# SBUF offsets of the matmul operands in a two-layer trunk: all tiles at one offset modulo 512 bytes

## The chip, the cores and the metric

The kernel runs on one core of a Trainium2 chip. The metric is the device time of one execution in microseconds (us), the median of several runs. Lower is better. A profile is one execution recorded by the hardware profiler; its span runs from the first to the last instruction of the program.

## The reference

A sequence of 512 tokens, 1024 wide, goes through two layers. Each sub-layer's output is added to `alpha * h` and normalised. Layer 0 mixes tokens with a Mamba-2 scan (SSD), layer 1 with stick-breaking attention; each is followed by an MLP with a squared ReLU and 4096 hidden units.

```
for layer in range(DEPTH):                 # DEPTH = 2
    if layer < N_A_LAYERS:                 # layer 0
        mix = mamba2_mixer(h, w_in, conv_w, ..., w_out)
    else:                                  # layer 1
        k, v = shared_kv(h, sb_w_k, sb_w_v)
        mix = stick_breaking_attention(h, sb_w_q, k, v, sb_w_o)
    h = layer_norm(DEEPNORM_ALPHA * h + mix, ...)
    h = layer_norm(DEEPNORM_ALPHA * h + square(relu(h @ w1)) @ w2, ...)
```

All values are float32.

## The kernel before

**Precision.** Every float32 matrix is split into a high part (float32r) and a low part, and every product is three matmuls: high by high, high by low, low by high. This is `mm3`, lines 207 to 209. Nearly every line of TensorE in the profile is one of these three. Each matmul has a stationary operand of 128 x 128 and a moving operand of up to 512 columns, both read from SBUF. The stationary one is brought in by an instruction of its own, the weight load (PEld in the profile).

**Weights.** `stream` lists 272 weight pieces of 128 x 1024 float32 in the order of use. `emit_w` (lines 150 to 194) fetches piece number i into a raw tile (`wr`), ScalarE copies it to the high part `wh` (L190), VectorE or GpSimd subtracts to get the low part `wl` (L192). In the MLPs a second pool lends buffers: with `e = 2` extra ones, four pieces in a row go to the pool `wp`, the next two to the pool of the MLP, and so on (`use = ... i % (4 + e) >= 4`).

**Stages and their span in the trace.** SSD 0 to 471 us, MLP of layer 0 to 806, attention to 1100 (with the first part of the next MLP's work woven in), MLP of layer 1 to the end. Each MLP goes through the hidden units in four quarters q. First eight pieces of W1 give `f` (stationary `wh`/`wl`, moving the normalised activations `ln_hh`/`ln_hl`): 192 matmuls of 512 columns (in quarter 0 four pieces are done in halves of 256 columns). Then seven block products `P1` to `P7` with W2 (stationary the hidden activations `hP`/`lP`/`l`, moving `wh`/`wl`) are summed in the banks `X`, `Y`, `Z`, `V`: 168 matmuls of 512 columns. A scheduler sets the order of the instructions of each engine and the semaphores.

**Places in SBUF.** Each partition is filled from byte 16512 on, pool by pool, every tile rounded up to 32 bytes. In the kernel before this gives (last column: start modulo 512; every slice that a matmul reads starts a whole multiple of 512 bytes after its tile's start):

| pool | tiles | first byte | modulo 512 |
|---|---|---|---|
| `cp` | `ones_r`, `ident`, `tri_le`, `tri_gt`, `none_r`, `ntri_ge` | 16512 | 128 |
| `cp` | `mhalf` (4 bytes), `cw`, `cbias`, `hv`, `nw` | 19584 | 128 and others |
| `ap` | activations: `x_h`, `ln_hh`, `ln_hl`, `yT`, `R`, `L` (the `l` of the products), `v`, `o_h` | 20704 | 224 |
| `wp` | raw tiles, `wh`, `wl` (four buffers each) | 102624 | 224 |
| `lp` | `st`, `mv`, `rs`, `sm`, `nm`, `sq` of the norms: 608 bytes in all | 143584 | 224 and others |
| `sp`, `mlp0`, `att`, `mlp1`, one after the other | SSD: conv, `W`, `xd`, `bt`, `xe`, `yg`; MLP: `hP`, `lP`, lent `wh`/`wl`; attention: `q`, `k`, `sp`, `w`, `vp` | 144192 | 320 |

In the last SSD projection (`so`), two weight pieces lie in the free SSD buffers `xd`, `dx` and `yg` and are called `wx`, `wdx` and `wyg` in the profile; they are at 320, the pieces called `wh` and `wl` beside them at 224.

So each of the 7414 matmuls has a pair of offsets, moving and stationary. Of the 4566 matmuls of 512 columns 2672 have 224 and 224, 416 have 320 and 320, 14 have 128 and 128, and 1464 have two different ones (1216 moving 224 with stationary 320, 152 the other way round, 96 moving 320 with stationary 128). Of these 1464, 480 are `f` of the MLPs (twenty lent pieces of 24 matmuls, ten in each MLP), 816 are products of the MLPs, and 168 lie outside: 48 in `so`, 24 in the output projection of attention, 96 single ones between others. The 2848 shorter matmuls have equal offsets in 2272 cases and different ones in 576.

Of the kernel before, what the change touches and what calls it, by code (L numbers as in the profile page):

```python
# [11 lines left out]
F32 = mybir.dt.float32  # L12
# [5 lines left out]
P = 128  # L18
# [3 lines left out]
NT = T // P  # L22
DI = 2048
G = 8
H = 32
# [10 lines left out]
def trunk(ctx: ExitStack, tc: tile.TileContext, io):  # L36
    nc = tc.nc

    cp = ctx.enter_context(tc.tile_pool(name="cp", bufs=1))
    ap = ctx.enter_context(tc.tile_pool(name="ap", bufs=5))  # L40
    wp = ctx.enter_context(tc.tile_pool(name="wp", bufs=4))
    lp = ctx.enter_context(tc.tile_pool(name="lp", bufs=2))
# [11 lines left out]
    def f(x):  # L54
        return x.bitcast(F32)

    nc.scalar.preload_act_table_set("natural_log_exp_and_others")
    ones_r = cp.tile([P, P], F32R, name="ones_r")
    one = f(ones_r)
    nc.vector.memset(one, 1.0)  # L60
    warm = psum("bg", [P, 4, P], "warm")
    for _ in range(14):
# [11 lines left out]
    ntri_ge = cp.tile([P, P], F32R, name="ntri_ge")  # L74
    nc.gpsimd.affine_select(ntri_ge, f(none_r), pattern=[[-1, P]], compare_op=ALU.is_ge, fill=0.0,
                            base=0, channel_multiplier=1)
    mhalf = cp.tile([P, 1], F32, name="mhalf")
    nc.gpsimd.memset(mhalf, -0.5)
    cw = cp.tile([P, 32, 4], F32, name="cw")
    cb_ = cp.tile([P, 32], F32, name="cbias")  # L80
    hv = cp.tile([P, 3, H], F32, name="hv")
    nw = cp.tile([P, 16], F32, name="nw")

    stream = []
    marks = []
# [60 lines left out]
    sums = {}  # L146
# [75 lines left out]
    class Filler:  # L222
        def __init__(self):
            self.queue = []
            self.left = 0.0
# [85 lines left out]
    class Norm:  # L311
        def __init__(self, v, idx, name, final=False):
            self.v, self.idx, self.name, self.final = v, idx, name, final
            self.sums = idx % 2 == 1
            self.st = lp.tile([P, NT, 2, 6], F32, tag="st", name=f"{name}_st", bufs=2)
            self.mv = lp.tile([P, NT, 2], F32, tag="mv", name=f"{name}_mv", bufs=2)
            self.rs = lp.tile([P, NT], F32, tag="rs", name=f"{name}_rs", bufs=2)
            if self.sums:
                self.sm, self.nm, self.sq = (lp.tile([P, NT, w], F32, tag=f"s{w}{n}", name=f"{name}_{n}", bufs=1)
                                             for n, w in (("sm", 2), ("nm", 1), ("sq", 2)))  # L320
                self.junk = None
            self.hl = None
            self.rows = None

# [954 lines left out]
```

## Time and profile before

| | us |
|---|---|
| median of 3 runs (1435.85 to 1437.47) | 1436.23 |
| the profiled execution's time | 1436.23 |
| its span, first to last instruction | 1434.2 |
| TensorE busy (matmuls) | 1406.7 (98%) |
| VectorE busy | 1078.6 (75%) |
| ScalarE busy | 783.8 (55%) |
| GpSimd busy | 221.5 (15%) |

[...] What sets TensorE's pace is the distance from one start to the next, which is read from the timeline: the starts of the first matmul of a stretch and of the first one behind it, and how many lie between. Starts are printed to 0.01 us.

### The profile page before, as it was taken

How to read it: one execution, taken by the hardware profiler on the slowest of the kernel's cores; microseconds unless marked ns; L12 is line 12 of the kernel's file. 1: busy time of each engine (PE TensorE's matmuls, PEld its weight loads, DVE VectorE, ACT ScalarE, POOL GpSimd, SP SyncE). 2: the span in 40 equal slices, each digit the busy share in tenths (PEclk: the TensorE clock that was granted, in tenths of full speed). 3: DMA queues.
4: the chain of work that ended last, by engine and by line, in shares of the span. 5: the costliest groups of instructions: out<-in, count | busy, mean ns of one | idle time of the engine just before them, and what ended most of it. 6: DMA issues, size and time to landing. Idle time of an engine off the chain costs nothing. (4 is left out here: it accounts for less than half of the span.)

```text
span 1434.2 us, 19323 instructions
## 1 busy us (share of the span) xinstructions
PE 1406.7 (98%) x7414; PEld 1200.9 (84%) x7414; DVE 1078.6 (75%) x1530; ACT 783.8 (55%) x1264; POOL 221.5 (15%) x249
## 2 busy tenths in 40 slices
PE   9999999999999999999999999999999999999997
PEld 6898897889997988888888789899879888888885
DVE  5798898368877696866759768787867966758587
ACT  5556574246652453636345468898833635354453
POOL 2344554135453100000000200000000000000001
PEclk9999999999999999999999999999999999999998
DMA  5223222221223455455453421121223454454533
GB/s 184 74 77 130 74 60 73 88 89 60 74 75 102 133 161 177 127 181 154 141 161 105 145 89 45 48 71 51 82 74 118 132 186 151 147 165 140 166 111 122
DMA packets 46699, 162.99 MB, mean 114 GB/s; under 512 B 5520, under 2 KB 5776, under 8 KB 46608
## 3 DMA queue, kind: packets, MB, share of 16 engines
q1 hardware_dynamic: 44016, 157.44, 35.1%
q10 hardware_dynamic: 2592, 4.33, 0.9%
q8 instruction: 58, 0.95, 0.3%
q14 instruction: 33, 0.27, 0.1%
HBM read 159.65 MB, written 2.10 MB: 113 GB/s over the span
## 5 line engine op out<-in xcount | busy, mean ns | idle before, releaser
L190 ACT CAST wh<-wr 128x1024 fp32r<-128x1024 f32 x235 | 246.6, 1050 | 336.1 <-DMA wr<-w 162.7
L192 DVE TENSOR_TENSOR wl<-wr,wh 128x1024 fp32r<-128x1024 f32 x218 | 268.3, 1232 | 181.7 <-ACT wh L190 180.7
L208 PE MATMUL f<-ln_hl,wh 128*128 128x512 f32 (+1 forms) x544 | 202.4, 373 | 0.0
L209 PE MATMUL f<-ln_hh,wl 128*128 128x512 f32 (+1 forms) x544 | 202.4, 373 | 0.0
L207 PE MATMUL f<-ln_hh,wh 128*128 128x512 f32 (+1 forms) x544 | 201.6, 373 | 0.0
L208 PEld LDWEIGHTS f<-ln_hl,wh 128*128 128x128 f32 x544 | 102.5, 189 | 18.7
L209 PEld LDWEIGHTS f<-ln_hh,wl 128*128 128x128 f32 x544 | 102.5, 189 | 18.6
L207 PEld LDWEIGHTS f<-ln_hh,wh 128*128 128x128 f32 x544 | 102.1, 189 | 18.7
L346 POOL TENSOR_TENSOR ln_rs<-ln_sq 128x1 f32<-128x1 f32 (+1 forms) x6 | 3.1, 510 | 643.5 <-ACT lnr L344 643.5
L207 PE MATMUL X<-wh,hP 128*128 128x512 f32 x192 | 75.6, 394 | 0.0
L208 PE MATMUL X<-wl,hP 128*128 128x512 f32 x192 | 75.5, 393 | 0.0
L209 PE MATMUL X<-wh,l 128*128 128x512 f32 x192 | 74.9, 393 | 0.0
L209 PE MATMUL pz<-wh,x_l 128*128 128x256 f32 x256 | 72.7, 284 | 0.0
L208 PE MATMUL pz<-wl,x_h 128*128 128x256 f32 x256 | 72.5, 283 | 0.0
L207 PE MATMUL pz<-wh,x_h 128*128 128x256 f32 x256 | 72.4, 283 | 0.0
L458 ACT CAST hP<-r 128x512 fp32r<-128x512 f32 x80 | 48.0, 619 | 31.2 <-DVE r L470 30.3
L192 POOL TENSOR_TENSOR wl<-wr,wh 128x1024 fp32r<-128x1024 f32 x17 | 42.5, 2502 | 93.8 <-ACT wh L190 93.4
L207 PE MATMUL px<-x_h,wh 128*128 128x512 f32 x128 | 50.7, 396 | 0.0
L208 PE MATMUL Y<-wl,hP 128*128 128x512 f32 x128 | 50.4, 394 | 0.0
L209 PE MATMUL px<-x_h,wl 128*128 128x512 f32 x128 | 50.2, 393 | 0.0
L208 PE MATMUL px<-x_l,wh 128*128 128x512 f32 x128 | 50.2, 392 | 0.0
L207 PE MATMUL Y<-wh,hP 128*128 128x512 f32 x128 | 49.8, 394 | 0.0
(1365 smaller groups left out, 3936.5 us busy)
## 6 DMA issues: line engine op xcount, KB each, us to landing
wr<-w SPq DMA_DIRECT2D x160, 512.0 KB, 3.6
wr<-w_bc SPq DMA_DIRECT2D x16, 512.0 KB, 3.5
wr<-w_x SPq DMA_DIRECT2D x16, 512.0 KB, 3.5
wr<-w_z SPq DMA_DIRECT2D x16, 512.0 KB, 3.6
wr<-w_so SPq DMA_DIRECT2D x16, 512.0 KB, 3.6
rawa<-w SPq DMA_DIRECT2D x16, 512.0 KB, 3.6
rawc<-w SPq DMA_DIRECT2D x16, 512.0 KB, 4.6
wr<-w_qk SPq DMA_DIRECT2D x16, 512.0 KB, 3.6
```

The lines of the kernel that those rows point to most:

```text
L190: nc.scalar.copy(hi, raw)
L192: eng.tensor_sub(lo, raw, f(hi))
L207: nc.tensor.matmul(out, a[0], b[0], start=start, stop=False, skip_group_check=skip)
L208: nc.tensor.matmul(out, a[0], b[1], start=False, stop=False, skip_group_check=skip)
L209: return nc.tensor.matmul(out, a[1], b[0], start=False, stop=stop, skip_group_check=skip)
L346: nc.gpsimd.tensor_add(rs, self.sq[:, t0:t1, 0], self.sq[:, t0:t1, 1])
L458: nc.scalar.copy(h, src)
```

## The change

Nothing is computed in another way. The small constants move ahead of the constant matrices, and the tiles of the norms take another shape and number, so that their sizes add up differently:

```
     nc.scalar.preload_act_table_set("natural_log_exp_and_others")
+    mhalf = cp.tile([P, 1], F32, name="mhalf")
+    cw = cp.tile([P, 32, 4], F32, name="cw")
+    cb_ = cp.tile([P, 32], F32, name="cbias")
+    hv = cp.tile([P, 3, H], F32, name="hv")
+    nw = cp.tile([P, 16], F32, name="nw")
     ones_r = cp.tile([P, P], F32R, name="ones_r")
...
-    mhalf = cp.tile([P, 1], F32, name="mhalf")
     nc.gpsimd.memset(mhalf, -0.5)
-    cw = cp.tile([P, 32, 4], F32, name="cw")
-    cb_ = cp.tile([P, 32], F32, name="cbias")
-    hv = cp.tile([P, 3, H], F32, name="hv")
-    nw = cp.tile([P, 16], F32, name="nw")
...
             self.sums = idx % 2 == 1
-            self.st = lp.tile([P, NT, 2, 6], F32, tag="st", name=f"{name}_st", bufs=2)
-            self.mv = lp.tile([P, NT, 2], F32, tag="mv", name=f"{name}_mv", bufs=2)
             self.rs = lp.tile([P, NT], F32, tag="rs", name=f"{name}_rs", bufs=2)
             if self.sums:
-                self.sm, self.nm, self.sq = (lp.tile([P, NT, w], F32, tag=f"s{w}{n}", name=f"{name}_{n}", bufs=1)
-                                             for n, w in (("sm", 2), ("nm", 1), ("sq", 2)))
+                x = lp.tile([P, NT, 14], F32, tag="sums", name=f"{name}_sums", bufs=1)
+                self.sm, self.nm, self.sq = x[:, :, 0:2], x[:, :, 2:3], x[:, :, 4:6]
                 self.junk = None
+            else:
+                self.st = lp.tile([P, NT, 2, 6], F32, tag="st", name=f"{name}_st", bufs=1)
+                self.mv = lp.tile([P, NT, 2], F32, tag="mv", name=f"{name}_mv", bufs=1)
```

What it does to the places: the six constant matrices start at 17632 (224 modulo 512) instead of 16512 (128). `ap` and `wp` stay where they were. `lp` holds 512 bytes instead of 608, so that the pools of the stages start at 144096 (224) instead of 144192 (320). In the changed program all 7414 matmuls have a moving and a stationary operand at 224. A few tiles that no matmul reads have other offsets before and after: `yl` and `sz` of the SSD, the sums of the norms.

What it does to the program: nothing else. On each of the five engines the built programs have the same instructions in the same order with the same waits and the same semaphore updates; only addresses differ, and `sm`, `nm` and `sq` are called `sums` with a step of 56 bytes from token tile to token tile.

## Rows read from the trace of the kernel before

**Rows 1.** The page, part 1: span, and busy time of each engine.

```profile
span 1434.2 us, 19323 instructions
PE 1406.7 (98%) x7414; PEld 1200.9 (84%) x7414; DVE 1078.6 (75%) x1530; ACT 783.8 (55%) x1264; POOL 221.5 (15%) x249
```

**Rows 2.** Table by stretch: us, busy time (count) by engine, granted clock, DMA share, GB/s.

```profile
600.00:700.00 100.00, 100.00 (x436) 81.65 (x435) 74.37 (x90) 48.18 (x64) 0.00 (x0) 1.00 0.47 146
```

**Rows 3.** Waits of PE over the span: us, times, longest; the first row.

```profile
PE ln_b L394 <- DVE v L430: 2.5, 1, 2.5
```

**Rows 4.** Timeline, last SSD projection, weights in two pools: start, duration, line, tiles.

```profile
453.06 0.39 PE L207 MATMUL so<-wh,yT4h 128*128 128x512 f32 x1
...
457.82 0.40 PE L207 MATMUL so<-wx,yT4h 128*128 128x512 f32 x1
...
460.64 0.39 PE L207 MATMUL so<-wdx,yT4h 128*128 128x512 f32 x1
```

**Rows 5.** Timeline, W1 of quarter 1, MLP of layer 0: two lent pieces, then four others.

```profile
567.66 0.39 PE L207 MATMUL f<-ln_hh,wh 128*128 128x512 f32 x1
...
578.91 0.39 PE L207 MATMUL f<-ln_hh,wh 128*128 128x512 f32 x1
...
600.67 0.40 PE L207 MATMUL X<-wh,hP 128*128 128x512 f32 x1
```

**Rows 6.** Timeline of the weight loads at the start of the four pieces.

```profile
578.91 0.19 PEld L208 LDWEIGHTS f<-ln_hl,wh 128*128 128x128 f32 x1
```

**Rows 7.** Timeline, the products `V` (P2) and `Y` (P3) of quarter 1.

```profile
629.78 0.40 PE L207 MATMUL V<-wh,hP 128*128 128x512 f32 x1
...
634.00 0.39 PE L207 MATMUL Y<-wh,hP 128*128 128x512 f32 x1
...
639.46 0.39 PE L207 MATMUL f<-ln_hh,wh 128*128 128x512 f32 x1
```

**Rows 8.** Timeline, starts of the products of quarters 0, 2, 3 and the row behind.

```profile
517.83 0.40 PE L207 MATMUL X<-wh,hP 128*128 128x512 f32 x1
...
556.76 0.40 PE L207 MATMUL f<-ln_hh,wh 128*128 128x512 f32 x1
...
683.38 0.39 PE L207 MATMUL X<-wh,hP 128*128 128x512 f32 x1
...
722.48 0.39 PE L207 MATMUL f<-ln_hh,wh 128*128 128x512 f32 x1
...
766.75 0.40 PE L207 MATMUL X<-wh,hP 128*128 128x512 f32 x1
...
805.68 0.38 PE L394 MATMUL ln_b<-ident,v 128*128 128x128 f32 x2
```

**Rows 9.** Timeline, products of quarter 0 in the MLP of layer 1.

```profile
1135.47 0.40 PE L207 MATMUL X<-wh,hP 128*128 128x512 f32 x1
...
1174.39 0.40 PE L207 MATMUL f<-ln_hh,wh 128*128 128x512 f32 x1
```

**Rows 10.** Timeline, matmuls of 256 columns: the gate projection of the SSD.

```profile
100.06 0.28 PE L209 MATMUL pz<-wh,x_l 128*128 128x256 f32 x1
...
101.48 0.28 PE L209 MATMUL pz<-wh,x_l 128*128 128x256 f32 x1
```

**Rows 11.** Timeline, matmuls of attention with a constant matrix as the stationary operand.

```profile
903.19 0.28 PE L1120 MATMUL z<-sp200l,ntri_ge 128*128 128x256 f32 x1
903.31 0.22 PE L1120 MATMUL z<-sp200h,ntri_ge 128*128 128x128 f32 x1
```

**Rows 12.** Groups of VectorE, 495 to 805 us: count, busy us, mean ns, idle before.

```profile
L459 DVE TENSOR_TENSOR lP<-r,hP 128x512 fp32r<-128x512 f32 x24 | 16.0, 683 | 0.0
L459 DVE TENSOR_TENSOR l<-r,hP 128x512 fp32r<-128x512 f32 x16 | 10.9, 682 | 1.2 <-ACT hP L458 1.2
```

**Rows 13.** Table by stretch, PE alone: the granted clock behind an idle TensorE.

```profile
241.80:245.20 3.40, 3.40 (x9) 0.50 0.51 154
```

## The prediction

> **What bounds the kernel now.** First the busy times: TensorE has matmuls in flight in 98% of the span, the next engine, VectorE, is at 75% [rows 1]. Then the table by stretch: in the MLP from 600 to 700 us TensorE is busy in all 100 us, at the full granted clock (1.00), with 436 matmuls, and VectorE has a quarter of its time left [rows 2]. Then the waits: the longest that TensorE has in the whole span is 2.5 us, for the rows of a norm, outside the MLPs' flow [rows 3]. So in the MLPs the time is the number of matmuls by the distance from one start to the next. A change of that distance goes into the end one for one; a change on any other engine does not.
>
> The program is the same before and after, instruction by instruction and wait by wait. The one question is whether a matmul's pace hangs on where its operands lie. The timeline answers it, since the kernel before mixes places within a stage. In the last SSD projection, 21 matmuls with `wh`/`wl` (moving at 224, stationary at 224) go from 453.06 to 457.82 us: 4.76 / 21 = 226.7 ns. The 12 behind them take `wx` (moving at 320, same stationary tiles) from 457.82 to 460.64: 235.0 ns [rows 4]. In the MLP, the moving operand stays and the stationary one changes place: 48 matmuls with two lent pieces (320 against 224) take 567.66 to 578.91, 11.25 / 48 = 234.4 ns; the 96 behind them (224 and 224) take 578.91 to 600.67, 21.76 / 96 = 226.7 ns [rows 5].
>
> That alone could mean that 320 is a bad place. The products say no. The 18 matmuls of `V` from 629.78 to 634.00 have moving 224 and stationary 320: 234.4 ns. The 24 of `Y` behind them have **both at 320**: 634.00 to 639.46, 227.5 ns [rows 7]. So it is the relation that counts: equal offsets are fast, different ones slow, by 7 to 8 ns in 227 (3%). A way in which it can come about is in sight: the weight load of the next matmul starts in the same hundredth of a microsecond as the matmul that runs (578.91 in both) and lasts 0.19 us [rows 5, 6], so the two operands are read side by side for most of a matmul. What collides there the trace does not show.
>
> [...]
>
> **The change part by part.** *W1 with lent pieces.* 480 matmuls `f` have different offsets and get equal ones: 480 x (234.4 - 226.7) = 3.7 us [rows 5].
>
> *Products.* A product's stationary operands are partly at 320 (`hP`, `lP`), partly at 224 (`l`), its moving ones at 224 or 320, so stretches of a few matmuls alternate and I cost a whole quarter: 168 matmuls. In the MLP of layer 0 the four quarters take 38.93 us (517.83 to 556.76), 38.79 (600.67 to 639.46), 39.10 (683.38 to 722.48) and 38.93 (766.75 to 805.68), together 155.75 [rows 5, 7, 8]. At 226.7 ns they would take 4 x 168 x 0.2267 = 152.3, at the 227.5 of the equal stretch in [rows 7] 152.9. The saving is 2.9 to 3.4 us. The other MLP repeats it: its first quarter takes 38.92 (1135.47 to 1174.39) [rows 9]. Twice: 5.7 to 6.8; I take 6.3, the middle.
>
> *Outside the MLPs.* 72 long matmuls in runs (`so`, output projection) by 235.0 - 226.7 give 0.6 us [rows 4]; 96 single ones could give 0.8 more. The 576 short ones with different offsets are in doubt: one with scores at 320 and a constant matrix at 128 has 0.12 us to the next start [rows 11], and the gate projection with both at 224 has 12 in 1.42 us, 118 ns [rows 10]. That is no difference within the print; taken at 3 ns either way it is -1.7 to +1.7 us. Outside together: -1.1 to +3.1. Long matmuls among short ones start anew each time, so I take little: 0.5.
>
> *Other engines.* Tiles of ScalarE, VectorE, GpSimd and the DMA queues move from 320 to 224 too. VectorE's `lP` (written at 320) takes 683 ns, its `l` (written at 224) 682 [rows 12]: nothing. The shared tile of sums has the same waits as the three tiles before, and the chain behind the last matmul has the same instructions: nothing.
>
> *Cover.* TensorE that runs 2.5% faster in the MLPs asks for weights 2.5% sooner. VectorE's 74% would be 76% [rows 2], so this costs nothing as long as the weights keep their lead; if not, see the second rival.
>
> Sum: 3.7 + 6.3 + 0.5 = **10.5 us**. The profiled execution took 1436.23 us, 2.0 more than its span, and is the median run; 1436.2 - 10.5 = 1425.7.
>
> **The rivals.** *It is the pool, not the offset.* Tiles at 224 are those of the pools that live for the whole program, tiles at 320 those of the stages' pools, so each fast stretch also has both operands in the same kind of pool. Were it a matter of regions, nothing would change: 1436.2. Against it: in the built program the fast pairs of [rows 5] lie up to some 70,000 bytes apart (`ln_hl` from byte 69856 on, `wl` at 139488), farther than the slow pairs of `V` in [rows 7], some 40,000 (`wh` at 123104, `hP` at 162624), and nothing marks a border at 144192 but the pools' own. [...]
>
> *The supply of weights takes back half.* If TensorE drains the weights faster than the chain of transfer, ScalarE and VectorE refills them, waits come up in the products. TensorE then runs at the pace of the supply, which is no slower than today's: half of the MLPs' gain would remain, about 1431. For it: VectorE at 74%. Against it: a TensorE busy for all of 100 us without a stall [rows 2].
>
> *Equal offsets collide with the other engines (slower).* With everything at 224, TensorE's reads could meet the reads and writes of VectorE and ScalarE, which today work half of the time at another offset. The price if it struck: the 2672 long pairs that are fast now would go from 226.7 to 234.4, 2672 x 7.7 ns = 20.6 us, and the slow ones would gain nothing: 1456.8. The whole is slower by more than 0.2% from the point on where it strikes a seventh of them (2.9 / 20.6). Against it: the 96 fast matmuls of [rows 5] run while both engines write pieces at 224 and at 320 in turn, with no change of pace.
>
> **How the numbers follow.** A measurement here tells 0.2% (2.9 us) from no change. Chances: the forecast 0.84, half taken back 0.06, the pool 0.06, the collision 0.04. The forecast's own range: products and outside at their ends give 3.7 + 5.7 - 1.1 = 8.3 to 3.7 + 6.8 + 3.1 = 13.6. A further doubt is the clock: behind an idle TensorE the granted clock was 0.50 for 3.4 us, which costs 1.7 us of progress [rows 13]; a stretch more or less of these shifts the end by as much. That makes 1422 to 1430, and since half taken back ends just above it and the other two are 0.10 together, this is the range. Faster: 0.84 + 0.06 = 0.90; within 0.2%: 0.06; slower: 0.04.
>
> **What would show it.** In the profile after: the `f` of lent pieces, and `V` of quarter 1, at about 227 ns from start to start, not 234; the products of a quarter in 38.1 to 38.3 us; `so` with `wx` at the pace of `wh`; TensorE still without waits in the MLPs, and durations of VectorE and ScalarE unchanged. The prediction is wrong if `V` stays at 234 with both operands at 224 (then the offset is not the cause), if the fast stretches of today slow down, or if waits for `wh` and `wl` appear in the products.

## The result, and the profile after

| | before | after |
|---|---|---|
| median of four runs each, same chip (us) | 1436.04 (1435.36 to 1437.47) | 1427.18 (1426.70 to 1427.62) |
| ratio after / before | | 0.9937, 95% interval 0.9920 to 0.9954 |
| profiled execution: time, span (us) | 1436.23, 1434.2 | 1426.79, 1424.7 |

The change makes the kernel 8.9 us faster, where 10.5 were forecast; 1427.18 lies inside the range. The page, part 1, of the kernel after stands against [rows 1], and one row of its table by stretch (us, busy time and count by engine, granted clock, DMA share, GB/s) against [rows 2]:

```profile
span 1424.7 us, 19323 instructions
PE 1394.1 (98%) x7414; PEld 1199.9 (84%) x7414; DVE 1078.2 (76%) x1530; ACT 783.9 (55%) x1264; POOL 221.4 (16%) x249
```

```profile
600.00:700.00 100.00, 100.00 (x443) 82.81 (x442) 75.19 (x91) 47.35 (x64) 0.00 (x0) 1.00 0.49 151
```

The busy shares say next to nothing: TensorE is at 98% in both. The count says it: 443 matmuls in the same 100 us instead of 436, at the same clock of 1.00. VectorE, ScalarE and GpSimd work for as long as before, within 0.4 us of some 1078, 784 and 221. So the matmuls of that stretch follow each other more closely on average, while the other engines do the same work.

The timeline of the kernel after (start, duration, engine, line, tiles; lines are one higher than before from the class of the norms on, while `mm3` keeps 207 to 209) shows where. First the last SSD projection, against [rows 4]: 21 matmuls with `wh`/`wl`, then 12 with `wx`, up to the first one with `wdx`.

```profile
452.17 0.39 PE L207 MATMUL so<-wh,yT4h 128*128 128x512 f32 x1
...
456.93 0.39 PE L207 MATMUL so<-wx,yT4h 128*128 128x512 f32 x1
...
459.65 0.39 PE L207 MATMUL so<-wdx,yT4h 128*128 128x512 f32 x1
```

The 21 take 4.76 us as before, 226.7 ns each; the 12 take 2.72, now 226.7 as well, where they took 235.0.

Then W1 of quarter 1 in the MLP of layer 0 (48 matmuls with lent pieces, 96 others), against [rows 5], and in the second piece the products `V` (18) and `Y` (24), against [rows 7].

```profile
565.32 0.39 PE L207 MATMUL f<-ln_hh,wh 128*128 128x512 f32 x1
...
576.20 0.39 PE L207 MATMUL f<-ln_hh,wh 128*128 128x512 f32 x1
...
597.96 0.39 PE L207 MATMUL X<-wh,hP 128*128 128x512 f32 x1
...
626.51 0.39 PE L207 MATMUL V<-wh,hP 128*128 128x512 f32 x1
...
630.59 0.39 PE L207 MATMUL Y<-wh,hP 128*128 128x512 f32 x1
...
636.03 0.39 PE L207 MATMUL f<-ln_hh,wh 128*128 128x512 f32 x1
```

Lent: 10.88 / 48 = 226.7 ns (before 234.4). Others: 21.76 / 96 = 226.7, unchanged. `V`: 4.08 / 18 = 226.7 (234.4). `Y`: 5.44 / 24 = 226.7 (227.5). There is one pace now.

The products of a quarter, against [rows 8]: quarters 0 and 2 from the first row to the second and from the third to the fourth.

```profile
516.36 0.39 PE L207 MATMUL X<-wh,hP 128*128 128x512 f32 x1
...
554.43 0.39 PE L207 MATMUL f<-ln_hh,wh 128*128 128x512 f32 x1
...
679.55 0.39 PE L207 MATMUL X<-wh,hP 128*128 128x512 f32 x1
...
717.63 0.39 PE L207 MATMUL f<-ln_hh,wh 128*128 128x512 f32 x1
```

They take 38.07 and 38.08 us, which is 168 x 0.2267. The table puts the whole span together, from the starts of the matmuls at the borders of the stages (after minus before, us; "again" is a second profile of the same changed kernel, taken later):

| part | after | again |
|---|---|---|
| SSD, up to 471 | -1.12 | -1.63 |
| MLP layer 0: W1, four quarters | -1.89 | -1.89 |
| MLP layer 0: products, quarters 0, 1, 2 | -0.86, -0.71, -1.02 | -0.86, -0.70, -1.02 |
| MLP layer 0: products, quarter 3 | 0.00 | -0.85 |
| attention, to the other MLP | +0.95 | +1.75 |
| MLP layer 1: W1 | -1.77 | -1.78 |
| MLP layer 1: products, quarters 0 to 3 | -0.84, -0.70, -1.02, -0.81 | -0.84, -0.70, -1.02, -0.81 |
| behind the last matmul | +0.35 | +0.33 |

The parts of each column add up to the difference of the unrounded spans, 9.4 and 10.0 us, a little more than lies between the medians. Two lines want an explanation: quarter 3, which gained nothing in one profile and all in the other, and attention, which loses in both.

**Quarter 3.** The products of quarter 3 begin at 761.15. The timeline there shows one wait of TensorE (in brackets: idle before, and who ended it), and VectorE's rows beside it show why.

```profile
764.10 0.39 PE L208 MATMUL X<-wl,hP 128*128 128x512 f32 x1
764.72 0.50 PE L209 MATMUL X<-wh,l 128*128 128x512 f32 x1 [0.23 <-DVE l L460]
```

```profile
762.84 1.22 DVE L192 TENSOR_TENSOR wl<-rawc,wh 128x1024 fp32r<-128x1024 f32 x1
763.98 0.68 DVE L460 TENSOR_TENSOR l<-r,hP 128x512 fp32r<-128x512 f32 x1
```

The low part `l` stood behind a weight piece (`wl`) on VectorE and ended at 764.66. The matmul that needs it started 0.62 us behind its forerunner instead of 0.23, and the next one 0.33 behind it: 0.50 us lost in two distances. In the profile "again" VectorE had it done by 761.84, two us before its matmul came at 763.8, and nothing waits:

```profile
761.16 0.68 DVE L460 TENSOR_TENSOR l<-r,hP 128x512 fp32r<-128x512 f32 x1
```

The rest of the missing 0.85 is at the other end: the last matmul of the quarter starts at 799.53 and the first of the norm behind it at 800.08, 0.32 later than a matmul's distance, since `ln_b` waits for `v` of VectorE. In "again" it follows at a matmul's distance (798.51 to 798.74), and the wait for `v` comes two transposes later, outside the quarter.

**Attention.** All of the loss of the profile after, 0.89 us, is there by 823 us, in the first hundred matmuls behind the MLP. The table by stretch for TensorE alone shows the clock (us, busy time and count, granted clock, DMA share, GB/s), first of the kernel after, then of the kernel before:

```profile
803.40:810.20 6.80, 4.74 (x22) 0.50 0.53 157
```

```profile
811.80:815.20 3.40, 3.40 (x17) 0.50 0.34 117
```

Both kernels let TensorE idle there for the norm. The longest wait is the same one, as [rows 3]:

```profile
PE ln_b L395 <- DVE v L431: 2.5, 1, 2.5
```

Before, 3.40 us of work ran at 0.50, after, 4.74 us. In the timeline of the kernel after, matmuls of 256 columns start 214 ns apart in that stretch (807.44 to 809.79, 11 distances) and 120 ns apart at 1.00 behind it (810.35 to 815.99, 47). Half of the difference, 0.67 us, is taken as lost progress, most of the 0.89: an estimate from the granted 0.50, a little above the 44% that these distances give.

### The profile page after: what moved, and what is told of

The parts are those of the page before. It is cut to its first block, busy times and chain, and to the rows that moved or that the text cites. A ratio compares the mean times of both kernels' runs of the same rounds, so it can differ in the third digit from the quotient of the medians.

```text
span 1424.7 us, 19323 instructions
## 1 busy us (share of the span) xinstructions
PE 1394.1 (98%) x7414; PEld 1199.9 (84%) x7414; DVE 1078.2 (76%) x1530; ACT 783.9 (55%) x1264; POOL 221.4 (16%) x249
## 5 line engine op out<-in xcount | busy, mean ns | idle before, releaser
L347 POOL TENSOR_TENSOR ln_rs<-ln_sums 128x1 f32<-128x1 f32 (+1 forms) x6 | 3.1, 523 | 635.3 <-ACT lnr L345 635.3
L208 PEld LDWEIGHTS pz<-wl,x_h 128*128 128x128 f32 x256 | 48.7, 190 | 0.9
```

Source lines behind the costliest of these rows:

```text
L208: nc.tensor.matmul(out, a[0], b[1], start=False, stop=False, skip_group_check=skip)
L347: nc.gpsimd.tensor_add(rs, self.sq[:, t0:t1, 0], self.sq[:, t0:t1, 1])
```

## The experiments

All are versions of the changed kernel and compute the whole reference. "At X" is the start of an operand modulo 512.

### How far apart, and modulo what

The tile of sums ends the pool `lp`, so its length sets where the pools of the stages start, while `ap` and `wp` stay at 224. Four lengths put `hP`, `lP`, the lent pieces and the rest of the stages' pools at a distance of 32, 64, 128 and 256 bytes from 224. With 16 in place of 14 (d32) they start at 256; with 18 (d64) at 288, with 22 (d128) at 352, with 30 (d256) at 480:

```
-                x = lp.tile([P, NT, 14], F32, tag="sums", name=f"{name}_sums", bufs=1)
+                x = lp.tile([P, NT, 16], F32, tag="sums", name=f"{name}_sums", bufs=1)
```

d32:

> The changed kernel with the tile of sums 32 bytes longer: stage pools at 256 modulo 512, the rest at 224; same instructions and waits. Theory A (operands must agree modulo 512): the lent f pieces of quarter 1 go back from 227 to about 234 ns from start to start, V of quarter 1 too, Y (both at 256) stays at 227; time about 1436. Theory B (the cost grows with the distance of the offsets): about 229 to 230 ns, time about 1430. Theory C (the pool, not the offset): nothing, as in the changed kernel, 1427.

d64:

> Sums 64 bytes longer: stage pools at 288, the rest at 224. Theory A (modulo 512): f lent and V at 234 ns, time about 1436. Theory A64 (agreement modulo 64 is enough): 227 ns everywhere, 1427. Theory B (grows with distance): between d32 and the kernel before, about 232 ns, 1433.

d128:

> Sums 128 bytes longer: stage pools at 352, the rest at 224. Theory A (modulo 512): f lent and V at 234 ns, time about 1436. Agreement modulo 128 is enough: 227 ns, 1427. Theory B: 234 ns or more, 1437.

d256:

> Sums 256 bytes longer: stage pools at 480, the rest at 224, as far apart as 512 allows. Theory A (modulo 512): f lent and V at 234 ns, time about 1436. Agreement modulo 256 is enough: 227 ns, 1427. Theory B: the slowest of the four, 240 ns or more, 1445.

The same two places as in [rows 5, 7], first in d32 and then in d256: lent `f`, other `f`, then `V` and `Y`.

```profile
568.99 0.39 PE L207 MATMUL f<-ln_hh,wh 128*128 128x512 f32 x1
...
580.19 0.39 PE L207 MATMUL f<-ln_hh,wh 128*128 128x512 f32 x1
...
601.96 0.39 PE L207 MATMUL X<-wh,hP 128*128 128x512 f32 x1
...
631.14 0.40 PE L207 MATMUL V<-wh,hP 128*128 128x512 f32 x1
...
635.35 0.40 PE L207 MATMUL Y<-wh,hP 128*128 128x512 f32 x1
...
640.80 0.39 PE L207 MATMUL f<-ln_hh,wh 128*128 128x512 f32 x1
```

```profile
566.24 0.39 PE L207 MATMUL f<-ln_hh,wh 128*128 128x512 f32 x1
...
577.12 0.39 PE L207 MATMUL f<-ln_hh,wh 128*128 128x512 f32 x1
...
598.88 0.39 PE L207 MATMUL X<-wh,hP 128*128 128x512 f32 x1
...
627.44 0.39 PE L207 MATMUL V<-wh,hP 128*128 128x512 f32 x1
...
631.52 0.39 PE L207 MATMUL Y<-wh,hP 128*128 128x512 f32 x1
...
636.96 0.39 PE L207 MATMUL f<-ln_hh,wh 128*128 128x512 f32 x1
```

| kernel | stages' pools at | distance to 224 | lent `f`, ns | `V`, ns | time, us |
|---|---|---|---|---|---|
| after | 224 | 0 | 226.7 | 226.7 | 1427.18 |
| d32 | 256 | 32 | 11.20 / 48 = 233.3 | 4.21 / 18 = 233.9 | 1437.14 |
| d64 | 288 | 64 | 233.3 | 233.3 | 1434.55 |
| before | 320 | 96 | 234.4 | 234.4 | 1436.04 |
| d128 | 352 | 128 | 232.3 | 232.8 | 1436.69 |
| d256 | 480 | 256 | 10.88 / 48 = 226.7 | 4.08 / 18 = 226.7 | 1427.73 |

The times of the four are single runs, beside a single run of the kernel before at 1435.63. Three things follow. The cost is all there at 32 bytes and does not grow, so theory B fails: 32 to 128 cost 5.6 to 7.7 ns a matmul. At 256 it is gone (226.7 ns), in every part of both MLPs, so theory A fails too: of the distances tried, the operands have to agree **modulo 256**, not modulo 512 as the change does it. And in d32 `Y`, whose two operands both lie in the moved pool at 256, runs at 5.45 / 24 = 227.1 ns right behind the slow `V`: the relation decides, not the place. From d32 to d256 only addresses differ, and 6.6 ns of 233.3 go.

### The two halves of the change

`lp_only` leaves the small constants behind the constant matrices, so that these stay at 128, and keeps the new tiles of the norms; `const_only` does the opposite, so that the stages' pools stay at 320.

The edit of `lp_only` against the changed kernel:

```
-    mhalf = cp.tile([P, 1], F32, name="mhalf")
...
-    nw = cp.tile([P, 16], F32, name="nw")
     ones_r = cp.tile([P, P], F32R, name="ones_r")
...
+    mhalf = cp.tile([P, 1], F32, name="mhalf")
...
+    nw = cp.tile([P, 16], F32, name="nw")
```

And that of `const_only`:

```
+            self.st = lp.tile([P, NT, 2, 6], F32, tag="st", name=f"{name}_st", bufs=2)
+            self.mv = lp.tile([P, NT, 2], F32, tag="mv", name=f"{name}_mv", bufs=2)
...
-                x = lp.tile([P, NT, 14], F32, tag="sums", name=f"{name}_sums", bufs=1)
...
+                self.sm, self.nm, self.sq = (lp.tile([P, NT, w], F32, tag=f"s{w}{n}", name=f"{name}_{n}", bufs=1)
+                                             for n, w in (("sm", 2), ("nm", 1), ("sq", 2)))
...
-            else:
-                self.st = lp.tile([P, NT, 2, 6], F32, tag="st", name=f"{name}_st", bufs=1)
-                self.mv = lp.tile([P, NT, 2], F32, tag="mv", name=f"{name}_mv", bufs=1)
```

`lp_only`:

> Only the norms' tiles changed: stage pools at 224, constant matrices still at 128. Theory (the MLPs hold the gain, 10.0 of 10.5 us): f lent, V and Y of quarter 1 at 227 ns, time 1427 to 1428, as the whole change. Rival (the constants in attention and the SSD matter as much): 1430 or more.

`const_only`:

> Only the constants moved: constant matrices at 224, stage pools still at 320 with the three tiles of sums. Theory: f lent and V stay at 234 ns, time 1435.5 to 1436.5, as the kernel before. Rival: 1433 or less.

`lp_only` took 1427.65 us (1425.74 to 1428.84; ratio to before 0.9939, interval 0.9921 to 0.9957), `const_only` 1435.50 (1434.91 to 1436.01; 0.9997, 0.9987 to 1.0006), against 1435.99 for the kernel before, timed beside them. The timeline of `const_only` at the place of [rows 5]:

```profile
567.36 0.39 PE L207 MATMUL f<-ln_hh,wh 128*128 128x512 f32 x1
...
578.60 0.39 PE L207 MATMUL f<-ln_hh,wh 128*128 128x512 f32 x1
...
600.36 0.40 PE L207 MATMUL X<-wh,hP 128*128 128x512 f32 x1
```

Lent pieces 11.24 / 48 = 234.2 ns, the others 21.76 / 96 = 226.7: as before. In each of the two MLPs all parts of `const_only` lie within 0.02 us of the kernel before. The whole gain is the stages' pools; moving the constant matrices from 128 to 224 brings nothing that can be told, although in `lp_only` 576 matmuls, 96 of them long ones among others, keep two different offsets.

### Is 224 a good place, or any common one

`common256` makes the constants 32 bytes longer, so that everything moves together from 224 to 256.

```
-    nw = cp.tile([P, 16], F32, name="nw")
+    nw = cp.tile([P, 24], F32, name="nw")[:, :16]
```

> The changed kernel with 32 bytes more behind the small constants: every operand of TensorE at 256 modulo 512, a multiple of 256. If only agreement counts: 227 ns everywhere, 1427, no difference from the changed kernel. If a start at a multiple of 256 bytes is better in itself (for TensorE's reads, or for the transfers and the other engines): less than 226.7 ns, or shorter transfers than 3.6 us.

It took 1427.52 us (1426.12 to 1429.09; ratio 0.9941, 0.9925 to 0.9956). The lent `f` of quarter 1 go from 566.01 to 576.89, 10.88 us, 226.7 ns each, and `V` takes 4.08 us, 226.7. In d32 the same value 256, in the stages' pools alone, was slow. Of these two values neither is good or bad by itself, and 1427.52 us against 1427.18 shows no gain from shorter transfers (3.6 us in the profiles before and after).

### Which of the reads collides

`low_off` puts only the lent `wl` at 320, by two gaps in the MLPs' pools, and leaves the lent `wh` and all else at 224. (These four lines make `mm3` lines 211 to 213 here.)

```
             hi = px.tile([P, 1024], F32R, tag="hi" + sfx, name=f"wh{i}", bufs=b)
+            if use:
+                pool.tile([P, 24], F32, tag="gap1", name=f"gap1_{i}", bufs=1)
             lo = px.tile([P, 1024], F32R, tag="lo" + sfx, name=f"wl{i}", bufs=b)
+            if use:
+                pool.tile([P, 104], F32, tag="gap2", name=f"gap2_{i}", bufs=1)
```

In `f` the order is L211 (stationary `wh`), L212 (`wh`), L213 (`wl`), with the moving operand always at 224. If it is the load of the next weights that meets the running matmul's reads, only the distance behind L212 is long, since `wl` is loaded beside it; if it is a matmul's own pair, only that behind L213.

> The changed kernel with the lent low parts (wl) of the MLPs' pool alone at 320, all else at 224: 160 of f have them as stationary operand, 144 products as moving one. In f each k goes high by high (L207), low by high (L208), high by low (L209). Theory load (the next weight load collides with the running matmul): the distance that grows is the one behind L208, whose matmul runs while wl is loaded; L207 and L209 stay at 227. Theory own (the matmul's own pair counts): the one behind L209 grows. Either way one in three of lent f is 5 to 20 ns slower and the time is about 1428 to 1429.

It took 1430.81 us in one run, between the two kernels and above the 1428 to 1429 expected. The timeline of the 48 lent matmuls:

```profile
565.88 0.39 PE L211 MATMUL f<-ln_hh,wh 128*128 128x512 f32 x1
...
577.03 0.40 PE L211 MATMUL f<-ln_hh,wh 128*128 128x512 f32 x1
```

11.15 / 48 = 232.3 ns: with one of the three stationary operands at another offset instead of all three, 5.6 ns of the 7.7 of [rows 5] are back. Over all lent groups of both MLPs the mean distance behind L212 is 231.4 ns (160 of them), behind L213 232.6 (160), and behind the next L211 233.5 (156), against 226.7 to 227.2 in the other pieces. So neither account holds alone: the third distance is the longest, and there neither the running matmul nor the load beside it has an operand at 320. The disturbance outlives the matmul that brings it. The ends of the ten lent groups show it in the same timeline: up to the first `wl` the distances are 226 to 227 ns, then 228 to 229 (behind the L212 beside which it is loaded), 230 to 231 (behind its own matmul) and 235 to 236; behind the matmul of the last `wl` comes 231, and four more stay long (235.8, 228.2, 232.6, 231.0 in the mean) before 226.4. Which read it starts from stays open.

### What the handover behind the MLP costs

Attention lost 0.8 us and more in each kernel with agreeing offsets so far, so the last experiment changes the wait at its start. The four blocks of transposes of the norm's last rows take their bank from the group `bg`, as other work does; in `turn_mm` the third and fourth block take one from `mm`. The edit is no more than that, but the scheduler also puts some instructions of TensorE, ScalarE and VectorE in another order, up to about 910 us. It was run five times beside the changed kernel itself.

```
-        def turn(self, grp):
+        def turn(self, grp, tags=("bg",) * 4):
...
-                pt = psum("bg", [P, 2, w], f"{nm}_b{mm}{t0}")
+                pt = psum(tags[mm], [P, 2, w], f"{nm}_b{mm}{t0}")
...
-                        product("P3", Y, False, mid=lambda: nxt.turn(rows[2]))
+                        product("P3", Y, False, mid=lambda: nxt.turn(rows[2], ("bg", "bg", "mm", "mm")))
```

`turn_mm`:

> The changed kernel, and at the end of the MLP of layer 0 the third and fourth block of transposes of tokens 0 to 255 go to a bank of the tag mm instead of bg, so that they don't wait for VectorE to empty Y. Theory handover (of the 10 us that the MLPs give, about 1 us is lost between 800 and 823 us, where TensorE waits 2.5 us for VectorE and the granted clock is 0.50 for 6.8 us instead of 3.4): the wait of 2.5 us goes, and with it the longer slow stretch; 1423 to 1425. Rival (the loss is elsewhere, or the next thing, ScalarE's and VectorE's copies of the norm, is just as late): 1427, as the changed kernel.

The changed kernel once more (`after_again`):

> The changed kernel once more, on the same chip beside the former: 1427 to 1427.5, ratio to the kernel before 0.9938 to 0.9944. Its trace tells whether the 0.95 us that TensorE lost to VectorE's low part at the start of the last products of the MLP of layer 0 come each time (theory: no, the two runs with the same operand offsets have 0.1 and 0.2 us there) and whether the slow stretch of 6.8 us comes each time (theory: yes, both had it).

`turn_mm` took 1425.56 us (1424.26 to 1426.58; ratio to before 0.9924, 0.9910 to 0.9938), the changed kernel 1427.45 (1426.20 to 1429.10; 0.9939, 0.9925 to 0.9953). It is 1.9 us faster by the medians, though the two intervals overlap, and lies between the 1423 to 1425 expected and the rival's 1427. The 2.5 us wait for `ln_b` is gone, but another one has come in its place. Its longest wait of TensorE, and the timeline there:

```profile
PE pv L209 <- DVE ln_hl L399: 3.0, 1, 3.0
```

```profile
802.89 0.28 PE L208 MATMUL pv<-wl,ln_hh 128*128 128x256 f32 x1
806.17 0.39 PE L209 MATMUL pv<-wh,ln_hl 128*128 128x256 f32 x1 [3.00 <-DVE ln_hl L399]
```

TensorE no longer stands before the transposes, and stands before the first product that needs their low part instead. Counted from the MLP's end, `turn_mm` is at the 19th matmul 0.7 us ahead of the changed kernel's first profile and 0.4 ahead of the second, not 2.5. Most of its gain lies 250 us later, in the clock, where both programs have the same order again. Late in attention both kernels wait equally long for the same tile; the changed one (its first profile, first row) goes on at half the clock, `turn_mm` (second row) at the full one, as the matmul's 0.78 and 0.50 us already tell.

```profile
1052.54 0.78 PE L1139 MATMUL o<-w712h,vp 128*128 128x512 f32 x1 [1.18 <-ACT w712h L1126]
```

```profile
1051.45 0.50 PE L1139 MATMUL o<-w712h,vp 128*128 128x512 f32 x1 [1.18 <-ACT w712h L1126]
```

The table by stretch at that place, first of the changed kernel, then of `turn_mm`, and last the second profile of the changed kernel, where the half clock lasts twice as long (`after_again`):

```profile
1052.60:1056.00 3.40, 3.40 (x8) 0.50 0.54 181
```

```profile
1051.40:1054.80 3.40, 3.13 (x12) 1.00 0.61 196
```

```profile
1050.10:1056.90 6.80, 6.40 (x14) 0.50 0.32 108
```

The second profile answers both questions put to `after_again`: the wait for `l` did not come again (of the 0.95 us that the expectation gives to it, 0.50 are that wait and 0.32 the quarter's end), and the 6.8 us stretch did not come in the same place; behind the MLP it was 3.4, against the theory.

Counted so for all profiles, what attention gained or lost follows the work done at 0.50. The table takes, between 800 and 1061 us, TensorE's busy time at that clock, half of its difference to the kernel before, and the measured difference of attention (from the MLP's last product to the first woven-in work of the next MLP, 14 us ahead of the border in the table of parts; so 0.84 here and 0.95 there):

| kernel | busy at 0.50, us | half of the difference | measured |
|---|---|---|---|
| before | 3.40 + 3.23 = 6.63 | | |
| const_only | 6.66 | 0.0 | +0.05 |
| d32 | 3.40 + 3.34 = 6.74 | +0.1 | -0.08 |
| d64 | 3.40 + 3.36 = 6.76 | +0.1 | -0.45 |
| low_off | 3.40 + 3.36 = 6.76 | +0.1 | +0.30 |
| d128 | 8.45 | +0.9 | +1.00 |
| after | 4.74 + 3.40 = 8.14 | +0.8 | +0.84 |
| common256 | 8.35 | +0.9 | +1.14 |
| lp_only | 9.09 | +1.2 | +1.77 |
| after_again | 3.40 + 6.40 = 9.80 | +1.6 | +1.64 |
| d256 | 9.88 | +1.6 | +1.76 |
| turn_mm | 3.40 | -1.6 | -1.40 |

In nine of the eleven the two agree within 0.3 us; in `d64` and `lp_only` 0.5 to 0.6 us stay open. So the clock goes with most of it. What decides whether a wait is followed by 3.4 us at 0.50, by 6.8 or by none is not settled: the same program had 6.8 + 3.4 in one profile and 3.4 + 6.8 in the other, and d128, whose offsets differ as in the kernel before, has the longer stretch as well.

## Why the prediction was right, and where it was off

**The pace.** The step from [rows 5, 7] to "equal offsets are fast" held in each place named ahead: lent `f`, `V`, and `so` with `wx` at 226.7 ns, products in 38.1 us; TensorE's one wait within the MLPs is that of quarter 3 (0.23 us idle), absent in the second profile. It held for the reason given, since addresses alone (d32 at 233.3 ns against d256 at 226.7) switch it on and off. It asked for more than is needed: in d256 tiles 256 bytes apart ran at the fast pace too. What collides, and why the cost reaches past the matmul at hand, the prediction left open, and it stays open.

**W1 with lent pieces**, forecast 3.7: the two MLPs give 1.89 + 1.77 = 3.7.

**Products**, forecast 6.3, between 5.7 and 6.8: the second profile gives 6.8 (all quarters of both MLPs), the upper end, because the common pace is 226.7 and not the 227.5 that `Y` showed in [rows 7]. The first gives 6.0, since 0.5 went to one wait for VectorE's `l` and 0.3 to the norm at the end of quarter 3.

**Other engines.** VectorE's groups between 490 and 800 us in the kernel after (count, busy us, mean ns, idle before), against [rows 12]:

```profile
L460 DVE TENSOR_TENSOR lP<-r,hP 128x512 fp32r<-128x512 f32 x24 | 16.0, 683 | 0.0
L460 DVE TENSOR_TENSOR l<-r,hP 128x512 fp32r<-128x512 f32 x16 | 11.0, 685 | 1.2 <-ACT hP L459 1.2
```

683 and 685 ns, from 683 and 682: nothing, as forecast. The prediction's cover was too cautious: TensorE asks for weights not 2.5% sooner in the MLPs but 1.6% (443 matmuls for 436), and VectorE's share is 75%, not 76.

**Outside the MLPs**, forecast a gain of 0.5 with ends at -1.1 and +3.1: this is the term that was mis-sized. It came out as a loss of 0.2 us in the first profile (-1.12 in the SSD, +0.95 in attention, +0.35 behind the last matmul), 0.5 in the second, 1.1 in `common256`, 1.8 in `lp_only`, 2.0 in `d256`. Its reason for taking so little, that long matmuls among short ones start anew each time, was an estimate that no run shows by itself: `lp_only`, where such pairs keep different offsets, took 1427.65 us, the whole change 1427.18. In the SSD the last projection, from 440 us on, gains 0.3 us in each of these five profiles (its 48 matmuls were 0.4 of the forecast) and 0.1 at most in the kernels at slow offsets. Most of the rest of the SSD's part comes in the first 30 us, where profiles of both kinds lie between -1.4 and +1.2, so it says nothing about the change. Behind the last matmul, which the forecast put at nothing, the five lose 0.2 to 0.5: VectorE works there without a pause over 0.43 us from 5 us ahead of that matmul on, and its first `v` from `Y` starts 0.27 us ahead of it instead of 0.64, so the end does not come as much sooner as the matmuls do. Attention's part is the half clock above. The prediction had that price, 1.7 us for a stretch more or less, but took it as a doubt to both sides; in the five profiles (`lp_only` with all but its constant matrices at agreeing offsets, `turn_mm` left aside) it went one way, by 0.8 to 1.8 us. That this is the difference between 10.5 and the measured 8.9 fits in size. Why it went one way was not found. Nor is the price paid everywhere. At the place of [rows 13] the kernel after has no slow stretch (granted clock 1.00), yet it gains under 0.2 us there, because TensorE now waits for `v` of VectorE, as it did not before:

```profile
248.01 0.50 PE L207 MATMUL so<-wh,yT0h 128*128 128x512 f32 x1 [1.60 <-DVE v L298]
```

The range's lower end, too, left the clock out: 1436.2 - 13.6 - 1.7 is 1420.9, not 1422.

**The rivals.** *It is the pool, not the offset* falls by the kernel after and d256, where pairs of different pools run at 226.7 throughout; d32, with the pools moved as in d256, is slow again in `V`. (That `Y` is fast in d32 would fit the pool as well.) *The supply of weights takes back half*: the nearest to it is the one wait of 0.5 us, for an `l` that stood behind a weight piece, and the second profile shows none of it; VectorE at 75% of the stretch keeps its lead. *Equal offsets collide with the other engines* falls by the 96 other `f` of the kernel after, still at 226.7.

## What to carry to other kernels

Where TensorE runs without waits, read the distance from start to start, not the durations (0.39 to 0.40 us at both paces here) or the busy share (98% before and after), and compare it between matmuls of one shape whose operands come from different pools: two paces in one profile are worth a look at the addresses. Here, of the distances tried, the moving and the stationary tiles wanted the same start modulo 256 bytes (226.7 ns at 0 and 256 bytes apart, 232.3 to 234.4 at 32 to 128); moving the pools to that cost no instruction and gave 0.6%. And when the long stretches become shorter, look again at the short waits between them: attention, where the granted clock fell to 0.50 behind them, took back up to 1.8 us of a gain of about 10.

## What the runs showed of the hardware that was not expected

- The price of different offsets was a step: 233.3 ns at 32 bytes apart, 232.3 to 234.4 up to 128, 226.7 at 0 and at 256.
- One operand out of place slowed its neighbours too: with `wl` alone at 320 (`low_off`), the distances behind all three matmuls of a group are 231.4 to 233.5 ns against 226.7 to 227.2 in the other pieces, the longest where neither operand at hand is out of place, and behind the last misplaced matmul's 231 ns four more distances stay long (228.2 to 235.8). Which read meets which was not settled.
- Behind waits of the same length (1.18 us) the granted clock was 0.50 in one kernel and 1.00 in another, and a stretch at 0.50 lasted 3.4 or 6.8 us in profiles of the same program. A stretch of 3.4 us at 0.50 cost under 0.2 us where a wait for another engine followed it.
